# Third modulation as row sums on VectorE: four chunks for both streams in the branch strips, eight during the first mixer's attention

## The chip, the cores and the metric

One NeuronCore of one Trainium2 chip runs the whole program. The metric is the time of one execution in microseconds (us), as the median of several. An execution has its own engines side by side: TensorE (PE in the profile, its weight loads PEld), VectorE (DVE), ScalarE (ACT), GpSimd (POOL), and SyncE (SP), whose queue issues nearly all weight transfers. Each engine works through its own queue in order; semaphores hold an instruction back until what it reads is there.

## The reference

Two transformer-like blocks on 256 latent tokens and 256 context tokens of 1024 channels. The first has two layers, each a mixer (a Fourier branch, a global attention of 8 heads, a window attention of 4, joined by gates) and an expert layer with 16 experts. The second block is a hybrid scan mixer and a gated MLP. What the change concerns are the modulations, which depend on the two conditioning vectors alone:

```python
mod   = silu_c  @ w_ada[l] + b_ada[l]     # latent stream; l = 0, 1
mod_c = silu_cc @ w_ada[l] + b_ada[l]     # context stream
m_lat = split(silu(c) @ w_mod[layer] + b_mod[layer], 6)             # second block: the third modulation
m_ctx = split(silu(c_ctx)[None] @ w_mod[layer] + b_mod[layer], 6)
h_lat = modulate_2(rms_norm_2(x_lat, norm_mix_pre), m_lat[0], m_lat[1])
h_ctx = modulate_2(rms_norm_2(x_ctx, norm_mix_pre), m_ctx[0], m_ctx[1])
x_lat = x_lat + m_lat[2] * ...            # m_lat[3..5] likewise; the context stream ends with the mixer
```

Each modulation is a vector of 1024 numbers times a matrix of 1024 x 6144. Of the third one the context stream needs only the first two of six parts, the latent stream all six.

## The kernel before

`build` (L1960) runs the first mixer, its expert layer `moe(0)`, the second mixer, `moe(1)`, and the second block. The program is written through a framework that plans each engine's queue: the source gives each operation its rank, and an operation whose inputs are ready may be planned ahead of a lower ranked or waiting one. So the order in a queue follows the source only roughly, and matmuls of one part stand between those of another.

The three modulations are kept in `modT[0..2]`, each 48 columns x 2 streams. A modulation is cut into twelve chunks of 512 outputs, (m, c) with m = 0, 1, 2 and c = 0 to 11; each is two loads of 1 MB. There are two ways to compute one:

- `mod_chunk` (L258) on TensorE, for both streams: 16 products per load with the silu vector as 32 narrow columns (L268), a copy by ScalarE (L271), four transposes, a reduction (L276) and the bias add (L278) on VectorE.
- `mod_chunk_v` (L280) on VectorE, for the latent stream alone: the weights come with outputs on partitions, and one multiply with a row of the silu vector, spread over all partitions, and a running sum (L290) give 128 outputs. Four such row sums and one bias add (L293) make a chunk. The row is spread by `bcast_cols` (L307): eight small matmuls (L313) and two copies (L315).

In the host's `_mod_blocks` (L1923) the first four chunks of a matrix are laid out for TensorE and the rest for row sums.

The first mixer (`mixer`, L548) goes: normalisation with four chunks of m = 0; five projections (L645 to L661) with the row sums (1, 4) to (1, 8) beside them, whose row lies in `oT[:, 0:2]`; the window attention (L663); the Fourier projection (L665); the global attention (L675); the Fourier branch (L677), whose outputs go into `oT[:, 0:2]`; and four "branch strips" (L694), where gates that are left are computed, the branch outputs are multiplied by their matrices and gated. All weights but the experts' pass through one ring of four buffers of 1 MB (`wraw`, L188).

In the two attentions, `fill` (L590) hands out other work after each step, in all `at` = 16 chunks and four gates: m = 0 chunks 4 to 11, then (1, 0) to (1, 3), then (2, 0) to (2, 3), all by `mod_chunk`. In the strips, `run_extra` (L699) spreads the remaining list over the gates: the row sums of (1, 9) to (1, 11) and of (2, 4) to (2, 11). For them `silu_row` (L691) makes two rows in tiles of the strips' pool.

Of the kernel before, what the change touches and what calls it, by code (L numbers as in the profile page):

```python
# [9 lines left out]
F32 = mybir.dt.float32  # L10
F32R = mybir.dt.float32r
BF = mybir.dt.bfloat16
# [5 lines left out]
D = 1024  # L18
# [100 lines left out]
class Kernel:  # L119
# [157 lines left out]
        b = self.V("b_ada", m) if m < 2 else self.V("b_mod")  # L277
        nc.vector.tensor_tensor(v, v, b[:, 4 * c:4 * c + 4].unsqueeze(2).to_broadcast([128, 4, 2]), op=OP.add)  # L278

    def mod_chunk_v(self, m, c):  # L280


        nc = self.nc
        src = self.a["w_ada"][m] if m < 2 else self.a["w_mod_2"]
        row = self.crow[0 if m < 2 else 1]
        acc = self.mp.tile([128, 4, 1], F32, name="modcol")
        for h in range(2):
            w = self.wraw(src[2 * c + h], 2, D)
            for k in range(2):
                nc.vector.scalar_tensor_tensor(w[:, k], w[:, k], 1.0, row, op0=OP.mult, op1=OP.mult,  # L290
                                               accum_out=acc[:, 2 * h + k])
        b = self.V("b_ada", m) if m < 2 else self.V("b_mod")
        nc.vector.tensor_tensor(self.modT[m][:, 4 * c:4 * c + 4], acc.to_broadcast([128, 4, 2]),  # L293
                                b[:, 4 * c:4 * c + 4].unsqueeze(2).to_broadcast([128, 4, 2]), op=OP.add)

    def mod_coef(self, m, i, gain, name, parts=1):

# [250 lines left out]
    def mixer(self, l, xsrc, extra):  # L548
# [8 lines left out]

        def run_extra(n):
            for _ in range(min(n, len(extra))):
                m, c = extra.pop(0)  # L560
                (self.mod_chunk_v if m and c >= 4 else self.mod_chunk)(m, c)

        gates = {}

        def silu_row(i, out):

            self.crow[i] = out
            self.bcast_cols(out, self.cst[i][:, :, 0])

        def gate(jj, i):  # L570
            w = self.wsplit(a["w_in"][l, 6 + 4 * i + jj])
# [9 lines left out]

        early = [(0, 0), (0, 1), (0, 2), (1, 0)]
        fills = [lambda x=x: gate(*x) for x in early]
        at = 16 if full else 0
        for n in range(at):
            fills.insert(n * (len(fills) - n) // at + n, lambda: run_extra(1))
        rate = max(0, len(fills) - 2) / (6 * T)
# [33 lines left out]
        with self.pool(f"at{l}", side="right") as self.ap:  # L621
# [38 lines left out]
            row_chunk()  # L660
            self.proj(l, 768, lambda t: kvg[:, t], range(4))  # L661
            row_chunk()
            self.attention(l, qw, kv, 2, T, lambda h, t: oT[:, 6 + h, t * 128:t * 128 + 128], fill, sink=sink)  # L663
            f = self.ap.tile([128, T, 256], F32, name="z4")
            self.proj(l, 0, lambda t: f[:, t], range(T))  # L665
# [19 lines left out]
        with self.pool(f"br{l}", side="right") as bp:  # L685
            ol = [bp.tile([128, KT, N], F32R, name=f"o{x}") for x in ("hi", "lo")]
            for k in (6, 7, 2, 3, 4, 5, 0, 1):
                self.split(ol[0][:, k], ol[1][:, k], oT[:, k])
            order = [(jj, i) for jj in range(4) for i in range(3)]
            load = [0 if x in early else 1 for x in order]  # L690
            if full:  # L691
                for i in range(2):
                    silu_row(i, bp.tile([128, D], F32, name=f"crow{i}"))
            for jj in range(4):  # L694
                for i in range(3):
                    if (jj, i) not in early:
                        gate(jj, i)
                    n = 3 * jj + i
                    run_extra(round(len(extra) * load[n] / max(1, sum(load[n:]))))  # L699
                w = self.wsplit(a["wbr"][l, jj])  # L700
                for _ in range(EARLY[jj] if not full else 0):
                    self.load_expert(l, FIRST + len(self.pre))
                for j in range(2):
                    d = jj * 2 + j
                    acc = None
                    for i, (b0, b1) in enumerate(((0, 2), (2, 6), (6, 8))):
                        ps = self.psum("mm")
                        for k in range(b0, b1):
                            self.mm3(ps[:, :N], [x[:, k, j * 128:j * 128 + 128] for x in w],
                                     [o[:, k] for o in ol], k == b0, k == b1 - 1)  # L710
                        m = bp.tile([128, N], F32, name="mt", bufs=3)
                        nc.vector.scalar_tensor_tensor(m, gates[jj, i, j], 1.0, ps[:, :N], op0=OP.add, op1=OP.mult)
                        if acc is not None:
                            nc.vector.tensor_tensor(mT[:, d] if i == 2 else m, m, acc, op=OP.add)
                        acc = m
            run_extra(len(extra))
# [1203 lines left out]
           "gla_bg_b_2", "d_skip_2"]  # L1920


def _mod_blocks(w):  # L1923

    n = w.shape[1] // 256
    t = w.T.reshape(n, 2, 128, D).transpose(0, 2, 1, 3).reshape(n, 128, 2 * D)
    return np.concatenate([_blocks(w[:, :2048], KT, 256), t[8:]])


def arrays(inp):  # L1930
# [10 lines left out]
        [inp["w_br_fourier"], _kv_rows(inp["w_br_global"], 2, 4), _kv_rows(inp["w_br_window"], 2, 2)], 1), KT, 256)  # L1941
    ada = inp["w_ada"]
    out["w_ada"] = np.stack([_blocks(ada[0], KT, 256), _mod_blocks(ada[1])])
    out["w_mod_2"] = _mod_blocks(inp["w_mod_2"][0])
    out["w_in"], out["w_out"] = _blocks(inp["w_in"], KT, 256), _blocks(inp["w_out"], KT, 256)
    for n in ("w_gate_e", "w_up_e", "w_down_e"):
        out[n] = _blocks(inp[n], 2, D)
# [12 lines left out]
def build(tc, a, dbg=None):  # L1960
# [4 lines left out]
    k.wps, k.sps = [k.wp], [k.sp]  # L1965
    with k.pool("modp", bufs=2, side="right") as k.mp:
        k.mixer(0, [a["x"], a["ctx"]],
                     [(0, c) for c in range(4, 12)] + [(m, c) for m in (1, 2) for c in range(4)]
                     + [(1, c) for c in range(9, 12)] + [(2, c) for c in range(4, 12)])
    k.moe(0, 2, 2)  # L1970
    k.dbg("xl0", k.X[0][:, 0])
    k.mixer(1, None, [])
# [23 lines left out]
```

## Time and profile before

| what | value |
|---|---|
| median of 3 runs | 2113.11 us (2112.95 to 2120.88) |
| the profiled execution | 2116.92 us, of it 2115.1 us span |
| TensorE busy | 1873.0 us, 89% |
| VectorE busy | 976.8 us, 46% |
| ScalarE busy | 564.5 us, 27% |
| DMA | 601.10 MB, mean 284 GB/s |

All times below count from the span's start. The first mixer's attentions begin at about 104 us (window) and 180 us (global); the strips run from 302 to about 432 us. Busy TensorE is not the same as TensorE at its peak, since matmuls are pipelined; the granted clock (PEclk) says how much of the full clock the engine was given, and the idle time of an engine counts only where the others wait for it.

### The profile page before, as it was taken

What the parts mean: (1) busy time and instruction counts of PE and PEld (TensorE: products, weight loads), DVE (VectorE), ACT (ScalarE), POOL (GpSimd) and SP (SyncE); (2) the same over time, 40 slices, a digit from 0 to 9 for tenths busy, and PEclk for the clock granted to TensorE, in tenths of its full rate; (3) what the DMA queues carried; (4) which work ended last, traced back from release to release, by engine and by line L of the source; (5) the groups of instructions that cost most, each with busy time, mean ns of one, the idle gap of its engine ahead of it and who ended that gap; (6) DMA issues with size and microseconds to landing.
All of it is one profiled execution on the core that took longest, in us unless ns stands there. A gap on an engine that the chain in (4) does not pass through costs nothing.

```text
span 2115.1 us, 30458 instructions
## 1 busy us (share of the span) xinstructions
PE 1873.0 (89%) x12678; PEld 1235.5 (58%) x12678; DVE 976.8 (46%) x1934; ACT 564.5 (27%) x1124; POOL 75.4 (4%) x97
## 2 busy tenths in 40 slices
PE   5989999997999999787899977788866669998998
PEld 3957778894443433224788953355422238897887
DVE  3875669653222232126776631221121138766564
ACT  4143532221011110004354410221100025345453
POOL 0210000000000000001200000000000000100000
PEclk9999999998999999999999987898786779998999
DMA  8745738755999999996315579999999983213551
GB/s 321 279 181 211 271 143 338 293 217 214 376 420 420 372 404 420 420 420 270 116 61 218 189 306 416 418 415 387 393 414 420 419 364 120 102 67 132 179 183 57
DMA packets 85450, 601.10 MB, mean 284 GB/s; under 512 B 10304, under 2 KB 11104, under 8 KB 13376
## 3 DMA queue, kind: packets, MB, share of 16 engines
q1 hardware_dynamic: 82928, 594.15, 70.7%
q10 hardware_dynamic: 1840, 4.67, 0.6%
q8 instruction: 100, 1.64, 0.3%
q0 software_dynamic: 544, 0.32, 0.2%
q14 instruction: 38, 0.31, 0.0%
HBM read 598.06 MB, written 1.05 MB: 283 GB/s over the span
## 4 chain that ended last, share of the span: by engine, by line
PE 70%; DMA 15%; DVE 7%; issue 4%; ACT 3%; POOL 1%; SPq 0%; DVEq 0%; POOLq 0%; ACTq 0%
PE ps L154 33%; PE ps L161 8%; PE ps L159 8%; PE ps L160 8%; DMA we<-w_down_e_dram 7%; DMA we<-w_up_e_dram 5%; PE ps L165 4%; PE ps L1848 4%; DMA we<-w_gate_e_dram 3%; PE ps L1849 2%; PE ps L268 2%; PE ps L1725 1%; PE ps L313 1%; POOL hr L206 1%; DVE xr L1073 1%
## 5 line engine op out<-in xcount | busy, mean ns | idle before, releaser
L154 PE MATMUL ps<-we 128*32 128x256 f32 (+2 forms) x2400 | 351.2, 528 | 85.8 <-DMA we<-w_up_e_dram 43.4
L154 PEld LDWEIGHTS ps<-we 128*32 128x32 f32 (+2 forms) x2400 | 121.0, 137 | 305.3 <-issue 134.6
L170 DVE TENSOR_TENSOR wlo<-w,whi 128x1024 fp32r<-128x1024 f32 x170 | 205.5, 1220 | 74.4 <-ACT whi L169 74.0
L154 PE MATMUL ps<-we,gT 128*32 128x256 f32 (+1 forms) x1536 | 203.5, 499 | 26.0 <-DMA we<-w_down_e_dram 25.4
L169 ACT CAST whi<-w 128x1024 fp32r<-128x1024 f32 x170 | 174.7, 1047 | 175.3 <-PE ps L160 92.4
L1047 DVE TENSOR_TENSOR we<-ps,we 32x512 f32<-32x512 f32 (+1 forms) x128 | 70.9, 554 | 194.6 <-PE ps L154 192.9
L154 PEld LDWEIGHTS ps<-we,gT 128*32 128x32 f32 (+1 forms) x1536 | 65.9, 127 | 134.4 <-issue 75.0
L159 PE MATMUL ps<-hhi,whi 128*128 128x512 f32 (+1 forms) x384 | 131.7, 343 | 0.1
L160 PE MATMUL ps<-hlo,whi 128*128 128x512 f32 (+1 forms) x384 | 131.7, 343 | 0.0
L161 PE MATMUL ps<-hhi,wlo 128*128 128x512 f32 (+1 forms) x384 | 129.9, 341 | 0.1
L1848 PE MATMUL ps<-hx,whi 128*128 128x512 f32 x352 | 125.7, 402 | 0.1
L154 PE MATMUL ps<-we,xg 128*32 128x256 f32 (+1 forms) x768 | 101.5, 493 | 5.4 <-DMA we<-w_gate_e_dram 3.6
L1014 DVE TENSOR_TENSOR g<-tanh,ps 128x512 f32<-128x512 f32 (+1 forms) x32 | 17.8, 555 | 184.5 <-PE ps L154 184.4
L1849 PE MATMUL ps<-hx,wlo 128*128 128x256 f32 x352 | 98.4, 283 | 0.0
L1012 DVE SCALAR_TENSOR_TENSOR tanh<-tanh,ps 128x512 f32<-128x512 f32 (+1 forms) x32 | 17.8, 555 | 164.5 <-ACT tanh L1011 164.5
L1011 ACT ACTIVATE tanh<-ps 128x512 f32<-128x512 f32 (+1 forms) x32 | 15.7, 489 | 288.3 <-PE ps L154 288.3
L161 PE MATMUL ps<-whi,hlo 128*128 128x256 f32 x320 | 91.7, 289 | 0.3 <-DVE hlo L367 0.3
L160 PE MATMUL ps<-wlo,hhi 128*128 128x256 f32 x320 | 91.0, 286 | 0.9 <-DVE wlo L170 0.9
L159 PE MATMUL ps<-whi,hhi 128*128 128x256 f32 x320 | 91.4, 287 | 0.3 <-ACT whi L169 0.3
L1022 ACT ACTIVATE gT<-ps 128x512 f32<-128x512 f32 (+1 forms) x32 | 15.7, 490 | 265.4 <-PE ps L165 265.4
L159 PEld LDWEIGHTS ps<-hhi,whi 128*128 128x128 f32 x384 | 73.3, 191 | 9.3 <-issue 1.3
L160 PEld LDWEIGHTS ps<-hlo,whi 128*128 128x128 f32 x384 | 73.3, 191 | 9.3 <-issue 1.9
(427 smaller groups left out, 3339.7 us busy)
## 6 DMA issues: line engine op xcount, KB each, us to landing
we<-w_gate_e_dram SPq DMA_DIRECT2D x128, 1024.0 KB, 11.8
we<-w_up_e_dram SPq DMA_DIRECT2D x128, 1024.0 KB, 11.4
we<-w_down_e_dram SPq DMA_DIRECT2D x128, 1024.0 KB, 12.8
w<-w_in_dram SPq DMA_DIRECT2D x53, 1024.0 KB, 5.1
w<-w_ada_dram SPq DMA_DIRECT2D x48, 1024.0 KB, 5.8
w<-w_mod_dram SPq DMA_DIRECT2D x24, 1024.0 KB, 6.3
w<-w_out_dram SPq DMA_DIRECT2D x12, 1024.0 KB, 4.9
w<-w_gate_dram SPq DMA_DIRECT2D x11, 1024.0 KB, 4.8
```

The costliest lines, as they stand in the source:

```text
L154: self.nc.tensor.matmul(ps, l, r, start=first, stop=last)
L159: mm(ps, l[0], r[0], start=first, stop=False)
L160: mm(ps, l[0], r[1], start=False, stop=False)
L161: mm(ps, l[1], r[0], start=False, stop=last)
L165: self.nc.tensor.transpose(ps, x, self.ident[:n, :n])
L169: self.nc.scalar.copy(hi, x)
L170: (eng or self.nc.vector).tensor_tensor(lo, x, hi.bitcast(F32), op=OP.subtract)
L206: self.nc.gpsimd.tensor_tensor(out, x, self.ex[:x.shape[0], e:e + 1].to_broadcast(list(x.shape)), op=OP.pow)
L268: nc.tensor.matmul(ps[32 * g:32 * g + 32, h * 256:h * 256 + 256], st[:, k], w[:, k], start=k < 4, stop=k >= 4)
L1047: nc.vector.tensor_tensor(op[e // 4 % 2][p:p + 32, s, j * W:j * W + W], ps[i, :W], gb[s][i, j * W:j * W + W], op=OP.mult)
L1848: nc.tensor.matmul(ps, l[0], hx[:, kk], start=kk == 0, stop=False, skip_group_check=True)
L1849: nc.tensor.matmul(ps[:, 0], l[1], hx[:, kk, 0], start=False, stop=kk == KT - 1, skip_group_check=True)
```

## The change

The whole third modulation is computed by row sums. Its four chunks 0 to 3 are needed for both streams; they are computed in the strips, by halves: `(2, c, h)` loads one megabyte and makes four row sums from it, two groups of 128 outputs for two streams. A first stream's product is written to a bf16 scrap tile `junk`, the second overwrites the weights. Its chunks 4 to 11, for the latent stream alone, move from the strips into the attentions, where the fills become 20 chunks and four gates: m = 0 chunks 4 to 11, and then four times one (1, c) on TensorE and two chunks of the third by row sums. For these a row of the second silu vector is spread into `oT[:, 0:2]` before the window attention. In the strips three rows are made in place of two. The host lays out all of `w_mod_2` for row sums.

```diff
-    def mod_chunk_v(self, m, c):
+    def mod_chunk_v(self, m, c, half=None):
...
-        row = self.crow[0 if m < 2 else 1]
-        acc = self.mp.tile([128, 4, 1], F32, name="modcol")
-        for h in range(2):
+        both = half is not None
+        i = 0 if m < 2 else 1
+        if half != 1:
+            self.acc = self.mp.tile([128, 4, 1 + both], F32, name="modcb" if both else "modcol")
+        acc = self.acc
+        for h in [half] if both else range(2):
             w = self.wraw(src[2 * c + h], 2, D)
             for k in range(2):
-                nc.vector.scalar_tensor_tensor(w[:, k], w[:, k], 1.0, row, op0=OP.mult, op1=OP.mult,
-                                               accum_out=acc[:, 2 * h + k])
...
+                for s in range(1 + both):
+                    out = self.junk if both and s == 0 else w[:, k]
+                    nc.vector.scalar_tensor_tensor(out, w[:, k], 1.0, self.crow[i, s], op0=OP.mult, op1=OP.mult,
+                                                   accum_out=acc[:, 2 * h + k, s:s + 1])
+        if half != 0:
+            b = self.V("b_ada", m) if m < 2 else self.V("b_mod")
...
-                m, c = extra.pop(0)
-                (self.mod_chunk_v if m and c >= 4 else self.mod_chunk)(m, c)
+                m, c, *h = extra.pop(0)
+                (self.mod_chunk_v if m == 2 or m and c >= 4 else self.mod_chunk)(m, c, *h)
...
-        at = 16 if full else 0
+        at = 20 if full else 0
...
+            if full:
+                silu_row(1, oT[:, 0:2].rearrange("p k n -> p (k n)"))
             self.attention(l, qw, kv, 2, T, lambda h, t: oT[:, 6 + h, t * 128:t * 128 + 128], fill, sink=sink)
...
-                for i in range(2):
-                    silu_row(i, bp.tile([128, D], F32, name=f"crow{i}"))
+                for i, r in ((0, 0), (1, 0), (1, 1)):
+                    silu_row(i, bp.tile([128, D], F32, name=f"crow{i}{r}"), r)
+                self.junk = bp.tile([128, D], BF, name="junk")
...
-    out["w_mod_2"] = _mod_blocks(inp["w_mod_2"][0])
+    out["w_mod_2"] = _mod_blocks(inp["w_mod_2"][0], 0)
...
-                     [(0, c) for c in range(4, 12)] + [(m, c) for m in (1, 2) for c in range(4)]
-                     + [(1, c) for c in range(9, 12)] + [(2, c) for c in range(4, 12)])
+                     [(0, c) for c in range(4, 12)] + [x for c in range(4) for x in [(1, c), (2, 2 * c + 4), (2, 2 * c + 5)]]
+                     + [(1, c) for c in range(9, 12)] + [(2, c, h) for c in range(4) for h in range(2)])
```

## Rows read from the trace of the kernel before

**Rows 1.** The page's chain of work that ended last: share by engine.
```profile
PE 70%; DMA 15%; DVE 7%; issue 4%; ACT 3%; POOL 1%; SPq 0%; DVEq 0%; POOLq 0%; ACTq 0%
```
**Rows 2.** Stretches: start:end, us, busy of PE, PEld, DVE, ACT, POOL (count), clock, DMA, GB/s.
```profile
180.00:302.00 122.00, 121.37 (x948) 85.95 (x948) 69.98 (x168) 57.43 (x129) 0.00 (x0) 1.00 0.57 216
204.00:235.00 31.00, 31.00 (x310) 21.46 (x309) 22.04 (x60) 17.69 (x44) 0.00 (x0) 1.00 0.71 272
235.00:244.00 9.00, 8.94 (x46) 7.36 (x45) 1.25 (x4) 1.68 (x3) 0.00 (x0) 1.00 0.33 118
244.00:273.00 29.00, 29.00 (x298) 19.84 (x299) 20.29 (x55) 16.82 (x40) 0.00 (x0) 1.00 0.79 294
273.00:302.00 29.00, 29.00 (x137) 21.06 (x136) 10.36 (x19) 9.66 (x17) 0.00 (x0) 1.00 0.27 106
302.00:432.00 130.00, 129.71 (x579) 106.55 (x577) 107.04 (x171) 33.23 (x42) 1.52 (x2) 1.00 0.77 297
```
**Rows 3.** VectorE's timeline (start, us, instruction, idle time before and releaser).
```profile
204.73 0.69 DVE L502 COPY PT<-ps 128x512 f32<-128x512 f32 x1 [7.78 <-PE ps L165]
...
282.63 0.29 DVE L510 COPY oT<-ps 128x128 f32<-128x128 f32 x1 [7.99 <-PE ps L154]
```
**Rows 4.** SP's timeline at the strips' end; the page's DMA issues (KB, us to landing).
```profile
418.52 0.33 SPq L796 DMA_DIRECT2D we<-w_gate_e_dram  x1
...
w<-w_mod_dram SPq DMA_DIRECT2D x24, 1024.0 KB, 6.3
```
**Rows 5.** Chain of waits within the global attention; busy time of L268 (PE, PEld, clock, DMA).
```profile
245.82 1.86 PE ps L268 x32
...
253.53 0.59 PE ps L165 x4
...
180.00:302.00 122.00, 22.40 (x320) 10.00 (x320) 1.00 0.57 216
```
**Rows 6.** VectorE's timeline in the strips; line L290 there (ns, first and last start).
```profile
318.70 1.22 DVE L290 SCALAR_TENSOR_TENSOR w<-w,crow 128x1024 f32<-128x1024 f32 x1
...
323.28 1.22 DVE L170 TENSOR_TENSOR wlo<-w,whi 128x1024 fp32r<-128x1024 f32 x1
...
L290 DVE SCALAR_TENSOR_TENSOR w<-w,crow x44: 1215/1221/1226, 306.4 to 406.0; 128x1024 f32<-128x1024 f32 x44
```
**Rows 7.** VectorE's groups, 180 to 302 us (count, busy us, mean ns, idle before).
```profile
L276 DVE TENSOR_REDUCE modT<-ps 128x8 f32<-128x32 f32 x10 | 1.9, 191 | 7.6 <-PE ps L165 7.5
L278 DVE TENSOR_TENSOR modT<-modT,vec 128x8 f32<-128x8 f32 x10 | 1.6, 157 | 0.0
```
**Rows 8.** Busy time by stretch: first mixer's projections, second mixer's global attention.
```profile
45.00:100.00 55.00, 54.18 (x450) 53.98 (x451) 48.70 (x90) 14.64 (x25) 10.55 (x12) 1.00 0.81 304
1080.00:1130.00 50.00, 48.06 (x366) 38.29 (x366) 42.00 (x79) 30.03 (x65) 0.00 (x0) 1.00 0.18 65
```
**Rows 9.** Spreading a row: chain of waits, and VectorE's timeline.
```profile
304.84 0.89 PE ps L313 x8
...
303.64 1.29 DVE L315 COPY crow<-ps 128x512 f32<-128x512 f32 x2
```
**Rows 10.** TensorE's timeline at the window attention's start.
```profile
110.66 0.47 PE L154 MATMUL ps<-kT,qT 128*128 128x512 f32 x1 [3.19 <-DVE qT L459]
```
**Rows 11.** VectorE's timeline at the program's start.
```profile
3.29 0.23 DVE L223 CAST identb<-ident 128x128 bf16<-128x128 f32 x1 [1.85 <-DMA ident<-ident_dram]
```
**Rows 12.** TensorE's timeline after a wait; a stretch of the second mixer.
```profile
153.12 1.93 PE L154 MATMUL ps<-PT,kvw 128*64 128x128 f32 x14 [1.70 <-DVE PT L502]
154.98 2.70 PE L268 MATMUL ps<-w,cst 128*32 128x256 f32 x30
...
161.60 1.93 PE L268 MATMUL ps<-w,cst 128*32 128x256 f32 x30
...
1050.00:1060.00 10.00, 7.00 (x25) 4.86 (x25) 8.95 (x24) 3.02 (x8) 3.84 (x5) 0.50 0.04 16
```

More of the change, by code (lines that the diff above doesn't have):

```diff
@@ L278, in mod_chunk @@
         nc.vector.tensor_tensor(v, v, b[:, 4 * c:4 * c + 4].unsqueeze(2).to_broadcast([128, 4, 2]), op=OP.add)
-    def mod_chunk_v(self, m, c):
+    def mod_chunk_v(self, m, c, half=None):
         nc = self.nc
         src = self.a["w_ada"][m] if m < 2 else self.a["w_mod_2"]
-        row = self.crow[0 if m < 2 else 1]
-        acc = self.mp.tile([128, 4, 1], F32, name="modcol")
-        for h in range(2):
+        both = half is not None
[4 more added lines that the diff above has]
+        for h in [half] if both else range(2):
             w = self.wraw(src[2 * c + h], 2, D)
             for k in range(2):
-                nc.vector.scalar_tensor_tensor(w[:, k], w[:, k], 1.0, row, op0=OP.mult, op1=OP.mult,
-                                               accum_out=acc[:, 2 * h + k])
-        b = self.V("b_ada", m) if m < 2 else self.V("b_mod")
-        nc.vector.tensor_tensor(self.modT[m][:, 4 * c:4 * c + 4], acc.to_broadcast([128, 4, 2]),
-                                b[:, 4 * c:4 * c + 4].unsqueeze(2).to_broadcast([128, 4, 2]), op=OP.add)
+                for s in range(1 + both):
[4 more added lines that the diff above has]
+            b = self.V("b_ada", m) if m < 2 else self.V("b_mod")
+            nc.vector.tensor_tensor(self.modT[m][:, 4 * c:4 * c + 4], acc if both else acc.to_broadcast([128, 4, 2]),
+                                    b[:, 4 * c:4 * c + 4].unsqueeze(2).to_broadcast([128, 4, 2]), op=OP.add)
     def mod_coef(self, m, i, gain, name, parts=1):
@@ L559, in run_extra, with silu_row @@
             for _ in range(min(n, len(extra))):
-                m, c = extra.pop(0)
-                (self.mod_chunk_v if m and c >= 4 else self.mod_chunk)(m, c)
+                m, c, *h = extra.pop(0)
+                (self.mod_chunk_v if m == 2 or m and c >= 4 else self.mod_chunk)(m, c, *h)
         gates = {}
-        def silu_row(i, out):
-            self.crow[i] = out
-            self.bcast_cols(out, self.cst[i][:, :, 0])
+        def silu_row(i, out, s=0):
+            self.crow[i, s] = out
+            self.bcast_cols(out, self.cst[i][:, :, s])
         def gate(jj, i):
@@ L1920, with _mod_blocks @@
            "gla_bg_b_2", "d_skip_2"]
-def _mod_blocks(w):
+def _mod_blocks(w, m=8):
     n = w.shape[1] // 256
     t = w.T.reshape(n, 2, 128, D).transpose(0, 2, 1, 3).reshape(n, 128, 2 * D)
-    return np.concatenate([_blocks(w[:, :2048], KT, 256), t[8:]])
+    return np.concatenate([_blocks(w[:, :256 * m], KT, 256), t[m:]]) if m else np.ascontiguousarray(t)
 def arrays(inp):
```

## The prediction

> **What bounds the kernel now.** I read the page's chain of work first: TensorE carries 70% of what ended last, VectorE 7% [rows 1]. The change lies inside the first mixer, so I cut that stage into stretches and read the busy table [rows 2]. From 180 us, where the first mixer's second (global) attention begins, to 302 us, where the strips' first branch matmul runs, TensorE is busy 121.4 of 122 us at the full granted clock (1.00, the 2.4 GHz level), while VectorE is busy 70.0. From 302 to 432 (the branch strips) TensorE is busy 129.7 of 130 and VectorE 107.0. So both stretches are TensorE's; VectorE has 52 us free in the first and 23 in the second. Within the first, VectorE is loaded unevenly: 22.0 of 31 us at 204 to 235, 20.3 of 29 at 244 to 273, but only 10.4 of 29 at 273 to 302. In between it stands still while a gate's matmuls run as a block: three idle times that end at 204.7, 243.7 and 282.6 us, the first of 7.78 us and the last of 7.99 [rows 3]. The reader should see that the free time comes mostly in a few large holes.
>
> **What follows the mixer passes the shift on.** The first expert weight is issued at 418.5 us [rows 4], after all loads of this stage, when the strips' tiles come free. Nothing after it is touched by the change, so I carry every us gained or lost before 432 us to the end one to one.
>
> **Removed from TensorE.** Four chunks of the third modulation no longer run there. A chunk is 32 narrow matmuls, 1.86 us in the chain, and four transposes, 0.59 us: 2.45 us [rows 5]. Four of them are 9.8 us, in a stretch where TensorE has no idle time: -9.8 us. The ten chunks that now lie between 180 and 302 us (320 matmuls [rows 5]) become five: four go, and one moves ahead into the first (window) attention, because `at` = 20 raises the fill rate from 18/24 to 22/24 per step. That move is neutral in the sum of TensorE's work.
>
> **Added to VectorE in the same stretch.** Eight chunks of four row sums come in: 32 instructions. One is shown as 1.22 us, but four in a row start within 4.58 us (318.70 to 323.28), so one costs 1.145 us: 36.6 us [rows 6]. Eight bias adds, priced by the like add at 0.16, are 1.3 us, less five chunks' reductions and adds, 0.19 + 0.16 each, 1.8 us [rows 7]. With 1.3 us for one more row's copies, below, VectorE's work there goes from 70.0 to 107.4 us. TensorE's goes from 122 to 122 - 5 x 2.45 + 1.8 = 111.5 us. To stay under TensorE, VectorE would have to be busy 96% of the time, and it is a queue in order: a softmax step behind a row sum waits up to 1.145 us, and TensorE's transposes behind that.
>
> How much that costs, no row shows; two rows bound it. In the second mixer's global attention, without any chunks, VectorE is busy 42.0 of 50 us (84%) and TensorE loses only 2 [rows 8]; while the five chunks run beside the projections of the first mixer it is busy 48.7 of 55 (89%) and TensorE loses 0.8 [rows 8]. At 84% the stretch would last 107.4 / 0.84 = 128 us, 16.4 over TensorE's need; at 96% or more, nothing. I take 91%, 118 us, nearer to the 89% row: the row sums wait for nothing but their weights and so fill holes which the softmax leaves, the three large ones among them. That is 6.5 us lost. About 2 of them come back, since matmuls that do not hang on the softmax (the Fourier stage, the next gate) are pulled into TensorE's waits: **+4.5 us**, with bounds 0 and 16.4.
>
> **The extra row ahead of the window attention.** `silu_row(1, ...)` issues two groups of eight matmul records, 0.89 us each, and two copies of 0.645 on VectorE [rows 9]. TensorE stands idle for 3.19 us at that place, until VectorE has made the queries [rows 10], so its 1.8 us fit into the hole; but the copies stand in VectorE's queue ahead of keys and queries: **+1.3 us** (bounds 0, if the queue has room, and 3.1).
>
> **The branch strips.** Row sums there stay 44 (three chunks of four, and 32 in the eight halves, before as well as after). One row more is spread: 1.8 us of TensorE, which has no hole here, and 1.3 of VectorE, which has: **+1.8 us** (bounds 0, if it slips into a wait before 302, and 3.1). The halves need 8 loads where the eight chunks needed 16, 1 MB each [rows 4]; the chunk loads move into the attention, whose DMA share is 0.57 [rows 2], and SP's queue holds the same 24 loads of this matrix in another order. All of them pass through the one ring of four buffers, so a gate's load now waits for a row sum to free a slot, which is one way in which the 16.4 us can come about. No transfer is saved and none is the bound: nothing for that. Sixteen row sums write bf16 scrap. The nearest row, a 128x128 cast to bf16, takes 0.23 us [rows 11]; no charge, and up to 0.1 us each (1.6 us) if the write were slower, inside VectorE's 23 free us.
>
> The Trainium skill, Vector Engine (DVE) Microarchitecture Reference, section "Points that are easy to get wrong", says that this class of instruction loses half its throughput when both SBUF sources are not bf16, which speaks against moving work to it. The 1.145 us per 1024 columns is the price with both sources fp32 [rows 6], and it equals that of the fp32 subtraction that follows at 323.28 (1.22 us shown, like the row sum). If the price were still to double, the sum would get another 36 us on VectorE.
>
> **Sum.** -9.8 + 4.5 + 1.3 + 1.8 = -2.2 us. The profiled execution took 2116.92 us, of which 2115.1 are the span and 1.8 lie around it; by the sum it would be 2114.7. It lies 3.8 us above the median of the runs, so against the median 2113.11 the forecast is **2110.9, say 2111 us**. About 0.5% (10.6 us) is what a measurement of this kernel can tell from no change; the forecast is no change.
>
> **Rivals.** (a) VectorE's work disappears wholly in the holes: -9.8 + 1.8 and up to 1.3: -8.0 to -6.7, 2105 to 2106 us. For it speaks that VectorE has 18.6 us free in the last 29 alone; against it that the chunks are spread over the steps before. Chance 0.17. Its lower end, with every bound at 0, is 2103.
>
> (b) VectorE becomes the bound of the global attention and TensorE's clock falls in the waits. The place is 204 to 273 us: VectorE's 43.6 us there [rows 2], with the 1.25 of the nine between, plus six to seven chunks of 4.6 (28 to 32 us) less 1.8 for five chunks are 70 to 74 us in 69, where TensorE needs 57. It decides once the holes of the gates are not reached because the gate's weights wait in the ring behind row sums. The price is the 84% row: +16.4. The rows show what follows a wait: after an idle time of 1.70 us before 153.1 us thirty narrow matmuls take 2.70 us, where the next thirty take 1.93, and in the second mixer a ten-us stretch with 7.0 us busy is granted 0.50, the 1.2 GHz level [rows 12]. Four such waits at 0.77 us are 3.1. -9.8 + 16.4 + 3.1 + 3.1 + 1.8 = +14.6: **2128 us**. For it: an even flow of softmax steps, each with four stops at VectorE. Against: the stretch 1080 to 1130 keeps 1.00 [rows 8]. Chance 0.2. This is the one that ends on the slower side.
>
> The Trainium skill, TensorE: Matmul & The Clock Gate, section "Why this matters for your kernels", also advises against idle gaps between bursts of matmuls for the sake of the clock; [rows 12] agree.
>
> (c) The row sum with two fp32 sources at half rate: VectorE 107.4 + 36.6 = 144 us in the stretch, at least 22 over the 122 of now: 2135 us or more. The 44 such instructions in the strips run at full rate [rows 6]; only the bf16 output is new. Chance 0.01.
>
> (d) The change does not do what it says: the planner puts the row sums behind the attention, into the strips. They can't go there, because the Fourier output overwrites the row that they read, but they could gather just before 302 us, where 18.6 us are free against 36.6: +18 - 9.8 + 3.1, 2124 us. Chance 0.04.
>
> **How the numbers follow.** The forecast (2106 to 2118) has 0.58, (a) 0.17, (b) 0.20, (c) 0.01, (d) 0.04. The range goes from (a)'s lower end, 2103, into the lower part of (b), 2125; some 0.18 stays outside. Faster by over 0.5% means under 2102.5, beyond even (a)'s bounds: 0.04. Slower by over 0.5%, above 2123.7: most of (b), (c) and half of (d), 0.17. Same: 0.79.
>
> **What would show it.** Right: the stretch from the global attention to the first branch matmul lasts 114 to 120 us with VectorE busy 88 to 94% of it and 160 narrow matmuls in it; the strips last 130 to 132 us. Wrong: TensorE waits of over 2 us for `st`, `PT` or `P` and granted clocks under 0.9 between 204 and 273 us (b); no waits and VectorE at 96% (a); a mean of row sums far from 1.22 us (c); a run of row sums alone just before the Fourier copies (d). The forecast as a whole is wrong if the stages after 432 us change in length, which I set to zero.

## The result and the profile after

The changed kernel takes 2127.32 us as the median of 4 runs (2126.63 to 2128.06), the kernel before 2113.1 us (2112.95 to 2120.88): 1.0058 times as long with all runs taken in, 95% interval 1.0041 to 1.0075 (the two medians alone make 1.0067). On another chip, beside experiments, it was 1.0045 (1.003 to 1.0061). So it is slower, by 0.3 to 0.75%; no change was forecast, 2111 us, and the time lies 2 us above the range. Nearest in time is rival (b), 2128 us.

The profiled execution took 2128.06 us, of which 2125.9 are span. The medians lie 14.2 us apart, the two profiled executions 11.1, of which 10.8 are span: the one of before lay 3.8 us above its median. What follows accounts for the 10.8. First its chain of work that ended last, to be read beside [rows 1]: followed back from the end, the chain covers only 43% of the span here, and breaks off before it comes to the first mixer. It says nothing of the loss.

```profile
PE 27%; DMA 9%; issue 3%; DVE 3%; ACT 1%; POOL 0%; DVEq 0%; POOLq 0%; ACTq 0%
```

So I cut the first mixer by events that both kernels have: last projection matmul, first score matmul of the window attention, first key transpose of the global attention, first and last branch matmul. Two rows of before, cut in this way (start:end, us, busy of PE, PEld, DVE, ACT, POOL, clock, DMA share, GB/s; compare [rows 2]):

```profile
179.00:301.90 122.90, 122.27 (x957) 86.68 (x956) 70.64 (x169) 57.64 (x129) 0.00 (x0) 1.00 0.56 214
301.90:429.50 127.60, 127.60 (x562) 104.71 (x562) 104.79 (x169) 31.06 (x39) 1.52 (x2) 1.00 0.76 295
```

The same view of the changed kernel: from the last projection matmul to the first score matmul, the global attention with the Fourier stage, two stretches within it, and the strips.

```profile
104.40:115.40 11.00, 8.31 (x75) 4.75 (x73) 7.62 (x17) 2.72 (x5) 3.93 (x4) 0.84 0.09 19
184.40:310.50 126.10, 114.33 (x774) 80.72 (x773) 104.75 (x233) 55.94 (x124) 0.00 (x0) 0.99 0.68 259
230.00:240.00 10.00, 7.65 (x72) 4.46 (x72) 10.00 (x28) 3.52 (x10) 0.00 (x0) 1.00 0.81 291
267.00:277.00 10.00, 5.95 (x40) 4.82 (x38) 10.00 (x24) 3.12 (x9) 0.00 (x0) 0.83 0.91 350
310.50:440.50 130.00, 130.00 (x581) 106.99 (x581) 106.07 (x165) 30.85 (x39) 1.52 (x2) 1.00 0.62 225
```

The 10.8 us of span divide so, rounded: ahead of the window attention 11.0 where before had 6.6 (104.0 to 110.7), +4.4; window attention 69.0 instead of 68.4, +0.6; global attention and Fourier stage +3.2; strips +2.4; the projections ended 0.4 later. Behind the strips next to nothing, -0.2: 1685.4 us to the end of the span, 1685.6 before. The first expert load shows the shift passed on, 418.52 in [rows 4]:

```profile
429.54 0.33 SPq L805 DMA_DIRECT2D we<-w_gate_e_dram  x1
```

The third row to look at is 230 to 240 us: VectorE has no idle time at all, and TensorE works 7.65 of 10. The reader sees the bound change hands there. It is not so in the whole stretch: the row sums run from 194.2 to 279.3 us, and the two rows of this part and of the part behind it are

```profile
194.20:279.30 85.10, 74.26 (x529) 53.06 (x530) 79.43 (x183) 38.46 (x90) 0.00 (x0) 0.98 0.78 295
279.30:310.50 31.20, 31.20 (x156) 22.56 (x155) 16.30 (x35) 12.03 (x24) 0.00 (x0) 1.00 0.41 160
```

While there are row sums VectorE is busy 93% of the time and TensorE is idle 10.8 us; behind them TensorE has no idle time, and VectorE is busy 16.3 of 31.2. What TensorE waited for in the 126.1 us (who waited, for whom, us in total, times, longest), where before waited once, 0.4 us:

```profile
PE ps L154 <- DVE PT L508: 6.5, 3, 4.0
PE ps L159 <- ACT whi L169: 2.0, 2, 1.3
PE ps L154 <- ACT P L491: 1.7, 4, 0.9
```

Where ScalarE is named, VectorE stands behind part of it: for `P`, ScalarE itself waited 22.7 us for VectorE's reductions (10.3 before). Weight loads ended hardly any wait, on VectorE a single one:

```profile
ACT P L491 <- DVE st L483: 22.7, 15, 4.9
...
DVE w L295 <- DMA w<-w_mod_dram: 1.2, 1, 1.2
```

The longest of TensorE's waits, in VectorE's timeline (start, us, instruction) and then TensorE's:

```profile
267.67 1.22 DVE L295 SCALAR_TENSOR_TENSOR w<-w,oT 128x1024 f32<-128x1024 f32 x1
...
271.11 1.22 DVE L295 SCALAR_TENSOR_TENSOR w<-w,oT 128x1024 f32<-128x1024 f32 x1
...
272.25 0.69 DVE L508 COPY PT<-ps 128x512 f32<-128x512 f32 x1
...
273.00 1.97 PE L154 MATMUL ps<-PT,kvg 128*64 128x128 f32 x14 [3.96 <-DVE PT L508]
```

A block of four row sums, 4.6 us, stands ahead of one copy of `PT`; TensorE has transposed already, has nothing else to do and waits 3.96 us. The granted clock is 0.50, the 1.2 GHz level, for 3.4 us after it (0.83 on average in the stretch 267 to 277).

The start, TensorE's timeline and then VectorE's (compare [rows 10]):

```profile
104.49 1.27 PE L319 MATMUL ps<-ident,cst 128*128 128x128 f32 x10
...
109.00 1.12 PE L165 MATMUL ps<-ident,kvw 128*128 128x128 f32 x4 [2.69 <-DVE oT L321]
...
115.41 0.49 PE L154 MATMUL ps<-kT,qT 128*128 128x512 f32 x1
...
108.26 1.28 DVE L321 COPY oT<-ps 128x512 f32<-128x512 f32 x2
```

The row's matmuls are done by 105.7, but VectorE copies the two results only at 108.26, behind head norms that were queued first, one of which holds VectorE idle for 1.55 us until GpSimd is done. Until then they occupy both of the PSUM buffers (`tp`) that key and query transposes use, so these wait 2.69 us, and then run at half clock: four transposes in 1.12 us instead of 0.60.

The row sums themselves are as priced (ns min/median/max, first and last start), bf16 scrap included:

```profile
L295 DVE SCALAR_TENSOR_TENSOR w<-w,oT x52: 1204/1219/1570, 50.3 to 278.1; 128x1024 f32<-128x1024 f32 x52
L295 DVE SCALAR_TENSOR_TENSOR w<-w,crow x28: 1214/1220/1227, 315.0 to 408.4; 128x1024 f32<-128x1024 f32 x28
L295 DVE SCALAR_TENSOR_TENSOR junk<-w,crow x16: 1218/1219/1226, 345.8 to 407.1; 128x1024 bf16<-128x1024 f32 x16
```

### The profile page after: what moved, and what is told of

The parts are those of the page before. It is cut to its first block, busy times and chain, and to the rows that moved or that the text cites. A ratio compares the mean times of both kernels' runs of the same rounds, so it can differ in the third digit from the quotient of the medians.

```text
span 2125.9 us, 30299 instructions
## 1 busy us (share of the span) xinstructions
PE 1873.1 (88%) x12566; PEld 1234.1 (58%) x12566; DVE 1014.4 (48%) x1998; ACT 563.8 (27%) x1120; POOL 75.3 (4%) x97
## 5 line engine op out<-in xcount | busy, mean ns | idle before, releaser
L159 PEld LDWEIGHTS ps<-hhi,whi 128*128 128x128 f32 x384 | 73.1, 190 | 11.1 <-ACT whi L169 2.7
## 6 DMA issues: line engine op xcount, KB each, us to landing
we<-w_gate_e_dram SPq DMA_DIRECT2D x128, 1024.0 KB, 11.8
we<-w_up_e_dram SPq DMA_DIRECT2D x128, 1024.0 KB, 11.3
we<-w_down_e_dram SPq DMA_DIRECT2D x128, 1024.0 KB, 12.7
```

The lines of the kernel that those rows point to most:

```text
L159: mm(ps, l[0], r[0], start=first, stop=False)
```

## The experiments

Theory: in the global attention it is VectorE's load as such that holds TensorE back; at the start it is the two PSUM buffers; in the strips the third row. The rivals: the order in VectorE's queue (blocks ahead of copies), the ring of weight buffers, the row's copies themselves, the halves in the strips. Behind the strips the same instructions took 1679 to 1691 us in the profiles of this study, so verdicts on a cause rest on the length of stretches. The window attention too took from 65.9 us (third row alone) to 68.4 (kernel before) with the same instructions, so the +0.6 above isn't read. Whole times are compared with the kernel before on the same chip.

**Row sums cut short** (changed kernel; row sums of the attention over 64 of 1024 columns, so the results of these eight chunks are left out).

```diff
-                    nc.vector.scalar_tensor_tensor(out, w[:, k], 1.0, self.crow[i, s], ...
+                    n = 64 if m == 2 and not both else D
+                    nc.vector.scalar_tensor_tensor(out[:, :n], w[:, k, :n], 1.0, self.crow[i, s][:, :n], ...
```

> The changed kernel with the 32 row sums of the attention's eight chunks cut to 64 of their 1024 columns (the result of these chunks is left out); loads, ring and order of the source stay. If VectorE's time for the row sums is what keeps the stretch from the global attention's key transposes to the first branch matmul at 126.0 us, it falls to TensorE's own need, 110 to 114 us, and no wait of over 1.5 us for VectorE is left in it. If the ring of four weight buffers or the lost cover of the four chunks on TensorE is the cause, it stays above 120 us.

2112.03 us (one run), before 2116.92 there. Stretch from the global attention to the first branch matmul:

```profile
181.10:292.90 111.80, 109.67 (x773) 78.32 (x772) 74.90 (x233) 55.67 (x124) 0.00 (x0) 1.00 0.75 292
```

111.8 instead of 126.1, with the same loads, queue and number of instructions (x233 on VectorE); no wait over 0.92 us is left. So the loads and the chunks that TensorE lost are not the cause: the 30 us of row sums are, and they cost 14.3 us, 9.6 as idle time of TensorE and 4.7 as longer busy time. A short sum also gives its ring buffer back sooner, so this run alone doesn't clear the ring; the waits of the changed kernel do, of which weight loads ended 1.8 us on TensorE, VectorE and ScalarE together. TensorE's 109.7 busy, 12.6 under before, also show that the five chunks of 2.45 are really gained.

**Blocks behind the copies** (changed kernel).

```diff
-            if n < len(steps):
-                fill()
             if old:
                 next(old)
+            if n < len(steps):
+                fill()
```

> The changed kernel with the attention's filling work ranked behind the copies of the transposed probabilities of the same step, not ahead of them: one pair of statements is swapped. VectorE's work is the same, 104.7 us in the stretch of 126.0. If runs of four row sums ahead of a copy that TensorE waits for are the cost (waits of 3.96 and 1.47 us for PT), those waits fall under 1 us and the stretch to 116 to 121 us: time down by 5 to 10 us. If it is VectorE's load as such (84% is all that an attention lets it reach), the stretch stays at 124 to 128 us and the waits move to other steps.

2126.41 us, 1.005 (1.0035 to 1.0065) of before. From the first score matmul to the first branch matmul 196.5 us, the changed kernel 195.1. The waits only move to the scaling of `P`, 7.5 us in all:

```profile
271.30 1.09 PE L165 MATMUL ps<-ident,P 128*128 128x128 f32 x4 [3.31 <-DVE P L501]
```

So which of the two ranks first does not decide. Row sums spread one by one were not tried.

**The attention's copies on ScalarE** (changed kernel).

```diff
-                (nc.vector.tensor_copy if v else nc.scalar.copy)(pt, ps[:, :len(kts)])
+                (nc.vector.tensor_copy if v and T < 4 else nc.scalar.copy)(pt, ps[:, :len(kts)])
-            nc.vector.tensor_copy(o(hg, t), ps[:, :128])
+            (nc.vector.tensor_copy if T < 4 else nc.scalar.copy)(o(hg, t), ps[:, :128])
```

> The changed kernel, but the first mixer's attentions make the second of the two PT copies of each step, and the copy of a head's output, on ScalarE instead of VectorE. In the global attention this takes 16 copies of 0.56 us and 16 of 0.29, 13.5 us, from VectorE's 104.7 and gives about as much to ScalarE's 60 of 126. Theory (VectorE's load as a whole is the cause of the 126.0 us): between the run with short row sums (VectorE 74.9 us, stretch 111.7) and the changed kernel (104.7, 126.0) the stretch grows by 0.48 us per us of VectorE; at 91.2 it should last about 119.5, some 6 us less, and the program should take 2120 to 2123 us. Rival (the blocks of row sums hold back single softmax steps, whatever the sum): the reductions and the scalings still stand behind the blocks of four, the stretch stays at 124 or more and the program over 2125. Second rival (ScalarE, which then does the casts of weights, the exponentials and all copies, becomes the next late engine): waits of TensorE for ScalarE's copies and casts of over 2 us, and no gain.

2116.6 us, 1.0007 (0.9995 to 1.0019) of before: the whole loss is gone. Stretch, and TensorE's waits in it:

```profile
179.10:296.60 117.50, 110.84 (x770) 78.41 (x769) 93.93 (x200) 64.63 (x156) 0.00 (x0) 1.00 0.74 278
...
PE ps L165 <- DVE P L501: 2.2, 3, 1.1
PE ps L154 <- ACT P L491: 1.7, 5, 0.9
```

10.8 us less VectorE, 8.6 us shorter; 119.5 was expected. Five unbroken blocks of four row sums stand in the queue, four in the changed kernel, and the longest wait for VectorE is 1.1 us, so this speaks for the load. It doesn't wholly clear the blocks, since the `PT` copies, for which TensorE had waited longest, no longer stand behind them. ScalarE, at 64.6 of 117.5, did not become late.

**The scalings on GpSimd as well** (the run before this one).

```diff
-                nc.vector.tensor_scalar(P[v], P[v], st[:, 4 + v:5 + v], None, op0=OP.mult)
+                if T == 4:
+                    nc.gpsimd.tensor_tensor(P[v], P[v], st[:, 4 + v:5 + v].to_broadcast([128, nk]), op=OP.mult)
+                else:
+                    nc.vector.tensor_scalar(P[v], P[v], st[:, 4 + v:5 + v], None, op0=OP.mult)
```

> The changed kernel with the attention's copies on ScalarE (as in the run of that name) and also the 32 scalings of P, 12.0 us on VectorE in the global attention, on GpSimd, which does nothing there. Theory (VectorE's load sets the stretch): VectorE falls from 94.0 to about 82 us, and by 0.48 us per us the global attention and the Fourier stage fall from 117.6 to about 112, near the 110.9 that TensorE is busy; the program 2 to 5 us under the run with the copies alone (2116.6), that is 2112 to 2115. Rival (latency: GpSimd takes 1 to 2 us for what VectorE does in 0.41, and the softmax chain waits for it): waits of TensorE for P of over 1 us in nearly every step, stretch over 120 and program over 2118. Second rival (GpSimd slows VectorE's instructions beside it): row sums longer than 1.22 us.

2127.15 us, 1.0053 (1.0039 to 1.0068) of before: the gain is lost again, and the theory's number missed. The stretch; two row sums beside two scalings and one behind them (VectorE, then GpSimd); a wait of TensorE:

```profile
183.70:307.40 123.70, 113.50 (x771) 80.98 (x770) 92.84 (x168) 65.28 (x156) 36.37 (x32) 0.96 0.70 264
...
194.78 2.05 DVE L295 SCALAR_TENSOR_TENSOR w<-w,oT 128x1024 f32<-128x1024 f32 x1
...
196.77 2.05 DVE L295 SCALAR_TENSOR_TENSOR w<-w,oT 128x1024 f32<-128x1024 f32 x1
...
198.75 1.22 DVE L295 SCALAR_TENSOR_TENSOR w<-w,oT 128x1024 f32<-128x1024 f32 x1
...
193.87 3.87 POOL L502 TENSOR_TENSOR P<-P,st 128x512 f32<-128x512 f32 x2 [23.87 <-DVE st L499]
...
124.99 0.66 PE L165 MATMUL ps<-ident,P 128*128 128x128 f32 x4 [1.50 <-POOL P L502]
```

VectorE lost 12 us of work and stayed 92.8 us busy (93.9 without the edit): a row sum beside a scaling on GpSimd takes 2.05 us instead of 1.22, and the scalings 1.94 each, where two elsewhere take 2.04 together. Both rivals hold: in this stretch TensorE waits 6.0 us for GpSimd's scalings. The Trainium skill, SBUF — State Buffer, section "SBUF: two separate sides", says that a VectorE instruction with two SBUF inputs and a GpSimd instruction that reads SBUF share a pair of ports, and that whichever starts first keeps it to its end. The rows agree: 1.99 us pass from the start of one row sum to that of the next, where a row sum of 1.145 and a scaling of 1.02 make 2.17.

**The row ahead of the window attention.** Alone (kernel before, row unused):

```diff
+            if full:
+                silu_row(1, oT[:, 0:2].rearrange("p k n -> p (k n)"))
             self.attention(l, qw, kv, 2, T, ...
```

> The kernel before with one thing added: the row of the second silu vector is spread into oT ahead of the window attention; nobody reads it. My forecast's price was 1.3 us (VectorE's two copies). The rival: the two copies stand in VectorE's queue behind work of less hurry, and until they run the row holds both PSUM buffers that the attention's first transposes need. Then the first score matmul, at 110.7 us before and 115.4 after the change, moves to about 115 us here (+4 to +5), TensorE waits over 2 us ahead of the key transposes, and the later stretches keep their lengths of before (global attention and Fourier 122.8 us, strips 127.7). By the forecast it moves to 112.0.

2119.58 us, before 2116.92 there. From the last projection matmul to the first score matmul 11.0 us as in the changed kernel, with the same wait:

```profile
107.95 1.12 PE L165 MATMUL ps<-ident,kvw 128*128 128x128 f32 x4 [2.69 <-DVE oT L315]
```

So the start's loss is the row's alone. Its copies on ScalarE (changed kernel; `bcast_cols` takes the copy as an argument):

```diff
-            nc.vector.tensor_copy(out[:, h * 512:h * 512 + 512], ps)
+            (copy or nc.vector.tensor_copy)(out[:, h * 512:h * 512 + 512], ps)
```

> The changed kernel with the two copies of that row made by ScalarE, which is idle there. If the held PSUM buffers cost the 4.7 us at the window attention's start, the first score matmul comes back from 115.4 to 110.7 to 112.5 us and the time falls by 3 to 4.7 us, to 2122.6 to 2124.3. If VectorE's load around that place is what costs (two copies less of 15 us), it falls by 1.3 us to 2126.

2126.8 us, 1.0043 (1.0029 to 1.0057); the wait stays, and the stretch is 9.1, so the copies' place brings back 1.9 of the 4.4 us:

```profile
106.60 0.69 PE L165 MATMUL ps<-ident,z 128*128 128x128 f32 x2 [2.54 <-ACT oT L321]
```

In the three PSUM buffers of scores and projections (kernel before, row unused):

```diff
-            ps = self.psum("tp")
+            ps = self.psum(tag)
...
+            if full:
+                silu_row(1, oT[:, 0:2].rearrange("p k n -> p (k n)"), tag="mm")
```

> The kernel before with one silu row more ahead of the window attention (unused), as in the run with the row alone, but its eight small matmuls write into the three PSUM buffers of the scores and projections instead of the two of the transposes. Theory (the wait of 2.69 us ahead of the first key transposes comes from the two transpose buffers, held until VectorE has copied the row): the wait goes or falls under 1 us, and the stretch from the last projection matmul to the first score matmul is at most 1.5 us longer than in the kernel before; the program within 2 us of it. Rival (the row's two copies in VectorE's queue delay keys and queries as such): a wait of about the same length stays, with another releaser, and the stretch stays 2.5 us or more longer.

2119.7 us (one run, of which 1690.7 behind the strips), before 2114.97. The transposes no longer wait for a buffer. They still stand behind 1.95 us of the row's matmuls, and the queries are waited for 3.60 us, 3.19 in [rows 10]; the first score matmul comes at 8.8 us:

```profile
101.95 1.95 PE L313 MATMUL ps<-ident,cst 128*128 128x128 f32 x16
...
110.64 0.60 PE L154 MATMUL ps<-kT,qT 128*128 128x512 f32 x1 [3.60 <-DVE qT L459]
```

Both theory and rival hold in part: 2.2 us are the held buffers, 2.2 the row's matmuls ahead of the transposes and its copies in VectorE's queue. With this edit and the copies of the attention on ScalarE:

> The changed kernel with both edits: the copies of the first mixer's attentions on ScalarE, and the extra row ahead of the window attention through the score buffers. Theory: the gains add, some 6 us from the first and 2 to 4 us from the second (2.69 us of wait and the half clock behind it), 2116 to 2120 us, still not under the kernel before. Rival (TensorE fills any wait with other work, so that gains do not add): no better than the better of the two alone.

2118.96 us, 1.0027 (1.0015 to 1.0039): no better than the attention's copies alone. The global attention is 117.8, but the wait of 3.60 is now followed by 6.8 us at half clock, and the window attention takes 71.5 us instead of 66.3. With the row's copies on ScalarE too:

> The run with the copies on ScalarE (2116.6) and the row through the score buffers with its copies on ScalarE, the scalings staying on VectorE. Theory: only the start differs from that run: 7.5 us or less from the last projection matmul to the first score matmul where it had 11.1, global attention and Fourier stage 117 to 118 us as there; 2112 to 2115. Rival: no gain, as with the score buffers and VectorE's copies (2118.96), because the wait moves to the queries and the clock falls there for longer.

2119.4 us, 1.0006 (0.9991 to 1.0021); 10.5 us to the first score matmul, not 7.5. ScalarE has made the first half of the queries by 109.67, behind the row's copies; VectorE makes the second half only at 113.46, behind head norms, rope and keys in its queue, with 1.38 us idle for GpSimd among them. Why these rank ahead here is not shown:

```profile
114.30 0.77 PE L154 MATMUL ps<-kT,qT 128*128 128x512 f32 x1 [5.24 <-DVE qT L465]
```

And with the scalings on GpSimd:

> The run before this one and also the row ahead of the window attention through the score buffers, with its two copies on ScalarE. Theory: neither the transposes' buffers nor VectorE's queue are held, so the first score matmul comes at most 7.5 us after the last projection matmul (kernel before 6.6, changed kernel 11.0, score buffers alone 8.8), and the program gains another 2 to 4 us: 2109 to 2113, under the kernel before. Rival (TensorE's 1.95 us for the row cannot be hidden there, or ScalarE is as late as VectorE): 8.5 us or more, no gain over the run without this edit.

2133.32 us, 1.0071 (1.0056 to 1.0086), the slowest of all, with the wait of 5.25 us at the start and GpSimd's in the attentions. No placing of the row at this point was free.

**The third row alone** (kernel before, unused).

```diff
+                self.bcast_cols(bp.tile([128, D], F32, name="crow2"), self.cst[1][:, :, 1])
```

> The kernel before with a third silu row made in the strips (unused). Theory: TensorE is busy all through the strips, so its eight more small matmuls of 0.112 us each per half, 16 in all, cost 1.8 us, and VectorE's two copies hide: strips 129.4 to 129.8 us where the kernel before has 127.7. The changed kernel has 130.1, the rest being one matmul trio more that the planner leaves there. Rival (the halves' 32 row sums with two rows and bf16 scrap, not the row, lengthen the strips): strips within 0.4 us of 127.7.

2115.44 us (one run), before 2114.97. Strips:

```profile
297.10:426.60 129.50, 129.50 (x579) 106.58 (x579) 106.37 (x171) 31.09 (x39) 1.52 (x2) 1.00 0.76 291
```

+1.9 by the row, of 2.4. The remaining 0.5 goes with two more matmuls in the strips (x581 against x579), and not with VectorE, since TensorE has no idle time there.

**The changed kernel again.**

> The changed kernel, unaltered, on the same chip as the three others, so that gains are read against it directly: 1.0058 times the kernel before, as measured, if the difference does not depend on the chip; 10 to 11 us above the run with the copies on ScalarE.

2126.75 us, 1.0045 (1.003 to 1.0061), 10.2 above the 2116.51 of before and some 10 above the run with the copies on ScalarE (2116.6, on another chip beside 2114.97). The stretch has the same shape:

```profile
184.10:311.50 127.40, 116.88 (x773) 82.85 (x772) 104.82 (x232) 55.76 (x124) 0.00 (x0) 0.95 0.67 256
```

**A smaller move.** Chunks 0 and 1 of the third modulation leave TensorE, and chunks 9 to 11 of the second become row sums in the attention, with the row that lies there since the projections, so that none is spread ahead of the window attention.

```diff
-                (self.mod_chunk_v if m == 2 or m and c >= 4 else self.mod_chunk)(m, c, *h)
+                (self.mod_chunk_v if m == 2 and c not in (2, 3) or m and c >= 4 else self.mod_chunk)(m, c, *h)
...
-        at = 20 if full else 0
+        at = 17 if full else 0
...
-            if full:
-                silu_row(1, oT[:, 0:2].rearrange("p k n -> p (k n)"))
...
-                for i, r in ((0, 0), (1, 0), (1, 1)):
+                for i, r in ((1, 0), (1, 1)):
...
-                     [(0, c) for c in range(4, 12)] + [x for c in range(4) for x in [(1, c), (2, 2 * c + 4), (2, 2 * c + 5)]]
-                     + [(1, c) for c in range(9, 12)] + [(2, c, h) for c in range(4) for h in range(2)])
+                     [(0, c) for c in range(4, 12)] + [(1, 0), (1, 9), (1, 1), (1, 2), (1, 10), (1, 3), (2, 2), (1, 11), (2, 3)]
+                     + [(2, c, h) for c in range(2) for h in range(2)] + [(2, c) for c in range(4, 12)])
```

> A version with less of the change: only chunks 0 and 1 of the third modulation are taken from TensorE, as halves in the strips (48 row sums there instead of 44, two rows as in the kernel before); to make room, the three chunks 9 to 11 of the second modulation are row sums in the attentions, and these use the row that already lies in place for the projections, so no row is spread ahead of the window attention. Theory (VectorE's share sets what the global attention loses): TensorE gives up 4.9 us; VectorE does about 84 us of 120 there, 70%, and between the runs at 57% (loss 0.6), 67% (2.1) and 80% (6.7 us) that is a loss of 2 to 3; the start as in the kernel before (6.6 us from the last projection matmul to the first score matmul), strips 127.7 to 128.5; in all 1 to 4 us under the kernel before. Rival (any row sum in the attention's queue costs more than the TensorE time it replaces): global attention and Fourier stage 123 us or more, program equal to the kernel before or above it.

2111.78 us beside 2115.66: 0.9984 (0.9972 to 0.9995). With the attention's copies on ScalarE:

> The run before this one with the attention's copies on ScalarE as well: VectorE falls to about 71 us of 119, 60%, loss about 1 us; global attention and Fourier stage 118 to 119.5; 2 to 5 us under the kernel before, and 1 to 2 under the run before this one. Rival (the copies on ScalarE delay the casts of weights and the exponentials once VectorE is not the late engine): no gain over the run before this one.

**2109.62 us, 0.9968 (0.9957 to 0.998): faster than both kernels.** Stretches of the first and of the second, global attention and strips:

```profile
176.00:296.90 120.90, 119.38 (x882) 83.82 (x881) 83.26 (x193) 56.83 (x127) 0.00 (x0) 1.00 0.60 235
296.90:425.70 128.80, 128.80 (x571) 105.74 (x571) 109.00 (x174) 31.05 (x39) 1.52 (x2) 1.00 0.72 276
```

```profile
176.10:293.50 117.40, 116.94 (x880) 82.86 (x879) 72.76 (x161) 65.64 (x159) 0.00 (x0) 1.00 0.63 242
293.50:422.60 129.10, 129.10 (x572) 105.95 (x572) 109.11 (x175) 31.12 (x39) 1.52 (x2) 1.00 0.72 275
```

The start is 6.6 us as before. The kernel before with the copies on ScalarE alone was not run, so how much of the second run's gain is the copies' is open; the first, without them, is 3.9 us under the kernel before. With these, TensorE's idle time (length less busy) stands against VectorE's share so, in the whole stretch and in the part from the first row sum of the attention to the last:

| kernel | VectorE busy / stretch | share | TensorE idle, us | share while row sums run | TensorE idle there, us |
|---|---|---|---|---|---|
| before | 70.6 / 122.9 | 57% | 0.6 | none | none |
| smaller move, copies on ScalarE | 72.8 / 117.4 | 62% | 0.5 | 65% of 58.8 | 0.2 |
| short row sums | 74.9 / 111.8 | 67% | 2.1 | 70% of 76.8 | 1.2 |
| smaller move | 83.3 / 120.9 | 69% | 1.5 | 73% of 61.6 | 1.3 |
| blocks behind the copies | 107.5 / 144.7 | 74% | 12.7 | 89% of 90.3 | 11.3 |
| scalings on GpSimd as well | 92.8 / 123.7 | 75% | 10.2 | 81% of 88.4 | 9.1 |
| copies on ScalarE | 93.9 / 117.5 | 80% | 6.7 | 91% of 78.0 | 5.2 |
| changed kernel, again | 104.8 / 127.4 | 82% | 10.5 | 93% of 85.8 | 9.6 |
| changed kernel | 104.8 / 126.1 | 83% | 11.8 | 93% of 85.1 | 10.8 |

The share of the whole stretch does not order the losses: with the blocks behind the copies 74% go with the largest, because its window attention ends some 17 us sooner, and work that lay there lies in this stretch. The share while row sums run does better. Two rows stay out of line even so. With the scalings on GpSimd, TensorE waits for GpSimd too; and the copies on ScalarE lose half as much at 91% as the blocks behind the copies at 89%. So the time of the row sums on VectorE is shown as the cause, but what VectorE's load does as such and what the place of single copies in its queue adds is not parted by these runs.

## Why the prediction was wrong, step by step

- **What bounds the kernel now: right.** TensorE's 9.8 us were really there to gain: with short row sums its busy time fell by 12.6 where five chunks of 2.45 are 12.25. Its need came to 109.7 us and not 111.5, since the 1.8 us of the extra row lie outside this stretch.
- **VectorE's work, 107.4 us: nearly right** (104.75), and its rate, 1.145 us per row sum, right; rival (c) fell.
- **"I take 91%, 118 us": the step that failed.** VectorE reached 83%, and the stretch 126.1 us. The term was +4.5 and is +14.3 (126.1 less the 111.8 with short sums). I spread one share over the whole stretch. VectorE did reach 93%, but only in the 85.1 us in which there were row sums; the last 31.2 us had none, and it was busy 52% of them. And at such a share an attention costs TensorE more than I took: 10.8 of 85.1 us. Of the two rows between which I chose, [rows 8], I took the one at 89%, the projections, because row sums wait for nothing and fill holes. But TensorE's projection matmuls need from VectorE only the low halves of the weights, made with each load, and a softmax step needs it four times. So 89% in the projections cost 0.8 of 55 us, and 91% in the attention with the copies on ScalarE 5.2 of 78. The row of the same kind, the second mixer's attention at 84%, gave 128 us and stood in the text as a bound. That it came so near 126.1 is in part chance: the same division gives 93.9 / 0.84 = 112 us for the copies on ScalarE, where 117.5 were measured. No run shows the "2 us that come back". Of the three large holes of [rows 3], two are gone, so that far the row sums did fill them; the last, 7.17 us up to 294.56, stayed empty, since the last row sum starts at 278.1.
- **The extra row, +1.3 with a bound of 3.1: missed, +4.4.** I counted the matmuls into TensorE's idle time and two copies into VectorE's queue. I did not ask which buffers the matmuls hold while they wait to be copied: both that the next transposes need, 2.2 us; and the half clock behind a wait of 2.69.
- **The strips, +1.8: +2.4**, of which the row 1.9. Direction and reason right.
- **Nothing after 432 us: right**, 1685.4 against 1685.6.
- **Rivals.** (b) named the cause, the place (204 to 273 us; waits of 6.5 us for `PT`) and, with 2128, the time. The time is in part luck: its terms for the attentions make +9.7, where +3.8 were measured, and its +14.6 stand against 10.8 between the profiled executions. Its clock term was too large: one period of 3.4 us at half clock, at most 1.7 us, where I took four waits and 3.1; the start took that place. Its chance, 0.2, was too low. (a) would have needed VectorE at 96% of the stretch. (d) is out: the row sums lie from 194.2 to 278.1, spread over the steps.
- **The ring of four buffers**, which I named as a way to the loss, is not one: in the changed kernel's stretch weight loads ended 1.8 us of waits on TensorE, VectorE and ScalarE together.

In sum: forecast -2.2, measured +10.8; of the 13.0 between them the attentions hold 9.1 (-5.3 forecast, +3.8 measured), the start 3.1, the strips 0.6, and 0.4 lie in the projections, less 0.2 behind the strips.

## What to carry to other kernels

Work that is moved off a full engine onto one that serves it step by step is not free up to 100%: here TensorE lost some 2 us of 112 to 121 at two thirds of VectorE, and 12 of 126 at 83%. Price the part of the stretch in which the work will really lie, here 85 of 126 us. Take the friction from a stretch with the same kind of dependence, not from the busiest row in sight, and unload the serving engine first (its PSUM copies to ScalarE) or move less. For each added matmul ask which PSUM buffers it holds until its copy comes up in the other engine's queue.

## What the hardware showed that I had not expected

- GpSimd is no free place for elementwise work beside VectorE: a row sum with two SBUF sources takes 2.05 us instead of 1.22 next to a scaling on GpSimd, and the scalings some 1.9 instead of 1.0.
- A bf16 result costs a row sum nothing either way: 1.219 us against 1.220.
- One wait can cost twice: 2.69 us idle ahead of 109.00, then 3.4 us at the 1.2 GHz level, in which four transposes take 1.12 us instead of 0.60; after a wait of 3.60 us it was 6.8 us in one run.
